# Order of the weight differences in a down projection, and of the token sums ahead of it

## The chip, the cores and the metric

The kernel runs on one core of one Trainium2 chip. The metric is the device time of one execution in microseconds (us); the median of several runs counts. Five engines work side by side and meet through semaphores: TensorE (PE) multiplies matrices, VectorE (DVE) and GpSimd (POOL) do elementwise work, ScalarE (ACT) does casts, copies and activations, and SyncE (SP) issues most transfers. Each engine works through its own queue in order, so an instruction that waits holds up all that stand behind it on that engine.

## The reference

The program computes two layers of a decoder trunk on 1024 tokens of width 1024. The change touches the dense feed-forward block that ends each layer:

```python
def swiglu(h, w_gate, w_up, w_down):
    return (jax.nn.silu(h @ w_gate) * (h @ w_up)) @ w_down

def reference(x, ...):
    h = x
    for layer in range(DEPTH):          # DEPTH = 2
        ...                             # norm and mixer, added to h
        n = rms_norm(h, norm2_g[layer])
        h = h + swiglu(n, ffn_w_gate[layer], ffn_w_up[layer], ffn_w_down[layer])
    return rms_norm(h, final_g)
```

All values are float32. The hidden width is 2816, that is 22 tiles of 128.

## The kernel before

**Exact products in three.** Every operand is cut into a high part (an ACT cast to the rounded matmul type) and a low part, the remainder (source minus high part, a subtraction on DVE or POOL). Each product is then three matmuls of 128x128 by 128x512: high by high, high by low, low by high. `vsplit` and `wsplit` do this for weights (low part on POOL, in `vsplit` always), `split` for activations (`pool_lo` chooses POOL or DVE for the low part). A DVE subtraction that forms such a remainder has line L358, a POOL one of a down weight L1370, its cast L1369.

**Seven products for eight.** The feed-forward block is multiplied in 2x2 blocks by a scheme of Winograd's kind: token halves are one side, neighbouring 128-wide feature tiles the other. With weight blocks a11, a12, a21, a22 the scheme needs S1 = a21 + a22, S2 = S1 - a11, a third difference a11 - a21 and a fourth one a12 - S2. On the activation side it needs four inner differences of each pair of hidden tiles.

**Early pairs.** The 22 hidden tiles are 11 pairs. For the first token half, `ffn_early` computes two products of each pair, for the gate and the up weights side by side: a half sum, which ACT copies out of PSUM into `u0` (line L1341 in `early`), and the full product, which the up weights' `up` in `uses` multiplies on DVE (L1241, kept as `last_up`). Meanwhile `form1` forms the sums and differences of the two token halves (`t1`, `t2`, `t3`, `t4`): `normed` (L1130) multiplies by the norm's factor `r` on DVE, `sub` (L1161) subtracts on DVE, `split` casts on ACT (L356) and forms the low part on DVE. `form1` is a generator; one step of it is written down after each early pair from pair 2 on.

**Late pairs.** `ffn_pair` computes the remaining five products of each pair. `form_down` forms the pair's four inner differences in its function `put` (line L1317, on DVE), splits them and stores them to `hc` in DRAM. For ten pairs that happens beside the next pair's products. The last pair's are written down inside `down`, as `rest`, in the first group, after its fourth product's operands are requested.

**Down projection.** `down` runs over three groups of hidden pairs (four, four and three pairs). In each group four pairs of output column tiles (`dps`) go through seven products in a fixed order: the plain first one, then S2, then a12 with the plain odd tiles (operand `ha` in the first group), the third difference, a22, S1 and the fourth difference. In a first loop S1 and S2 of all four are formed by `op`, which is `vop` on DVE (L1396); the loops of the second and third product form the third differences (`W[dp][2]`, in the place of a21) and the fourth (`W[dp][0]`, in the place of S2). The same line L1396 adds finished products to the residual `h`.

**Who sets the order.** The program is written in one order, but a planner places every engine's instructions by its own timeline: of what is ready it takes what comes first in the program, and what is ready early can be placed far ahead of its place in the program. `keep` fixes a transfer's place. `behind(i, first)` makes the planner put instruction `i` behind `first`; here it is used between instructions of one engine and adds no semaphore.

Of the kernel before, what the change touches and what calls it, by code (L numbers as in the profile page):

```python
# [13 lines left out]
ALU = mybir.AluOpType  # L14
# [9 lines left out]
NP = FT // 2  # L24
# [180 lines left out]
class Kern:  # L205
# [147 lines left out]

    def split(self, src, hi, lo, pool_lo=True):
        nc = self.nc
        nc.scalar.copy(hi, src)  # L356
        e = nc.gpsimd if pool_lo else nc.vector
        e.tensor_tensor(out=lo, in0=src, in1=hi.bitcast(F32), op=ALU.subtract)  # L358


    def rstd(self, h, r, tag="y"):
# [765 lines left out]
        return self.rstd(self.kt(self.h[hf]), self.t(pool, [P, HT], "rs", 1), tag)  # L1127

    def normed(self, out, hf, k, g, r):
        self.nc.vector.scalar_tensor_tensor(  # L1130
            out=out, in0=self.kt(self.h[hf])(k), scalar=self.col(g, k), in1=r, op0=ALU.mult, op1=ALU.mult
        )

# [7 lines left out]
                self.nc.sync.dma_start(self.bd[kk], f)  # L1141
                self.split(f, *self.X[nm][k], False)

    def form1(self, g, r, n8, cb, ft):

        nc = self.nc
        V = nc.vector
        X = self.X
        for nm in ("t1", "t2"):
            X[nm] = [self.hl(n8, k + 4 * (nm == "t1")) for k in range(4)]  # L1150
        for nm in ("22", "t4", "t3"):
            X[nm] = [[self.t(cb, [P, HT], "cb", 24, F32R) for _ in range(2)] for k in range(4)]
        n = 0

        def tmp():
            nonlocal n
            n += 1
            return self.t(ft, [P, HT], "ft", 4) if n % 2 else self.t(self.pp, [P, HT], "nq", 4)

        def sub(o, x, y):  # L1160
            V.tensor_tensor(out=o, in0=x, in1=y, op=ALU.subtract)  # L1161
            return o

        for k in range(4):
            b11, b21, b12, b22, t2 = (tmp() for _ in range(5))
            nc.sync.dma_start(b11, self.bd[k])
            nc.sync.dma_start(b21, self.bd[k + 4])
            self.normed(b12, 1, k, g, r)
            self.normed(b22, 1, k + 4, g, r)
            t1 = sub(b11, b12, b11)  # L1170
            self.split(sub(t2, b22, t1), *X["t2"][k], False)
            self.split(t1, *X["t1"][k], False)
            yield
            self.split(sub(b12, b22, b12), *X["t3"][k], False)
            self.split(sub(b21, b21, t2), *X["t4"][k], False)
            self.split(b22, *X["22"][k], False)
            yield
# [134 lines left out]
    def form_down(self, L, p, x, ts):  # L1312

        nc = self.nc

        def put(i, o, a, b):
            nc.vector.tensor_tensor(out=o, in0=a, in1=b, op=ALU.subtract)  # L1317
            t = ts[i in (2, 3)]
            self.split(o, t[:, 0, :], t[:, 1, :], p < NP - 1)
            d = (self.hc[L][p, i - 1], t.bitcast(F32))  # L1320
            if p == NP - 2 and i > 2:
                self.owed.append(d)
            else:
                (nc.gpsimd if p == NP - 2 else nc.sync).dma_start(*d)
            return o

        tmp = lambda: self.t(self.pp, [P, HT], "nq", 4)
        yield
        t1 = put(1, x["11"], x["12"], x["11"])
        yield  # L1330
        t2 = put(2, tmp(), x["22"], t1)
        yield
        put(4, tmp(), x["21"], t2)
        yield
        put(3, tmp(), x["22"], x["12"])
        yield

    def early(self, ps, w, u0, use):

        self.prod(ps, w[0](), self.X["11"], True, False)  # L1340
        self.nc.scalar.copy(u0, ps)  # L1341
        yield
        self.prod(ps, w[1](), self.X["21"], False, True)
        use("11", ps)
        yield
# [53 lines left out]
    def down(self, L, fp, fz, rest, X, first):  # L1399


        op, S = self.vop, self.nc.scalar
        h0, h1 = (self.kt(self.h[hf]) for hf in range(2))
        dps = range(KT // 2)
        j, ends = len(X), []

        def place():
            nonlocal j
            i, j = j % 12, j + 1
            if i >= 8:  # L1410
                return self.t(fp, [P, 2, HT], "ha", 4, F32R)
            return self.t(self.nb, [P, 2, HT], "n8", 8, F32R)

        def plain(hf, f):
            return self.plain8(L, hf, f, place(), self.t(fp, [P, HT], "hr", 4))

        for gi, g in enumerate(DGROUPS):
            n, ps = g[1] - g[0], range(*g)
            ta, tb = ("fffy", "mmrc")[:: 1 - 2 * (gi % 2)]
            s1, u0, a1 = [], [], []  # L1420
            W = [self.wdown(L, 0, g, fp, "wd0", 5)]
            X = X or [plain(0, 2 * p) for p in ps]
            W += [self.wdown(L, 2 * i, g, fp, "wd0", 5) for i in (1, 2, 3)]
            for i in dps:
                W[i] += self.wdown(L, 2 * i + 1, g, fp, "wd1", 5)
            A = [self.pst(t, [P, HT]) for t in ta]
            first += [self.vsplit(W[dp][0]) for dp in dps[len(first) :]]
            cast = self.last_cast
            for dp in dps:
                a11, a12, a21, a22 = W[dp]  # L1430
                self.prod(A[dp], first[dp], X, True, False)
                u0.append(self.t(fz, [P, HT], "u0", 4))
                self.behind(S.copy(u0[dp], A[dp]), cast)
                s1.append(op(self.wsum(fp, n, 4, 8), a21, a22))
                if ends:
                    self.behind(self.last_vop, ends[dp])
                a1.append(a11)
                W[dp][0] = op(self.wsum(fp, n, 4, 8), s1[dp], a11, ALU.subtract)
            X = [self.sums8(L, p, 2, place()) for p in ps]
            B = [self.pst(t, [P, HT]) for t in tb]  # L1440
            for dp in dps:
                self.prod(B[dp], self.vsplit(W[dp][0]), X, True, False)
                y = op(self.t(fz, [P, HT], "y", 2), B[dp], u0[dp])
                op(h1(2 * dp), h1(2 * dp), y)
                op(W[dp][2], a1[dp], W[dp][2], ALU.subtract)
            X = [plain(0, 2 * p + 1) for p in ps]
            for dp in dps:
                self.prod(A[dp], self.vsplit(W[dp][1]), X, False, True)
                op(h0(2 * dp), h0(2 * dp), A[dp])
                op(W[dp][0], W[dp][1], W[dp][0], ALU.subtract)  # L1450
            X = [self.sums8(L, p, 3, place()) for p in ps]
            for dp in dps:
                self.prod(B[dp], self.vsplit(W[dp][2]), X, False, False)
                y = op(self.t(fz, [P, HT], "y", 2), B[dp], u0[dp])
                op(h1(2 * dp + 1), h1(2 * dp + 1), y)
            X = [self.sums8(L, p, 4, place()) for p in ps]
            while self.owed:
                self.keep(self.nc.sync.dma_start(*self.owed.pop(0)))
            for _ in rest:
                pass  # L1460
            for dp in dps:
                self.prod(B[dp], self.vsplit(W[dp][3]), X, False, True)
                op(u0[dp], B[dp], u0[dp])
                op(h0(2 * dp + 1), h0(2 * dp + 1), u0[dp])
            X = [self.sums8(L, p, 1, place()) for p in ps]
            X6 = [plain(1, 2 * p + 1) for p in ps]
            if g[1] == NP:
                yield
            A = [self.pst(t, [P, HT]) for t in ta]
            for dp in dps:  # L1470
                self.prod(A[dp], self.vsplit(s1[dp]), X, True, False)
                op(h1(2 * dp + 1), h1(2 * dp + 1), A[dp])
            ends, first = [], []
            for dp in dps:
                self.prod(A[dp], self.vsplit(W[dp][0]), X6, False, True)
                op(h1(2 * dp), h1(2 * dp), A[dp])
                ends.append(self.last_vop)
            X = ()
        yield
# [208 lines left out]
def trunk(tc, A, out):  # L1688
    with ExitStack() as ctx:
        K = Kern(ctx, tc, A, out)  # L1690

        pq, gb, nb, ch = K.mixer0()
# [51 lines left out]
        def early(L, sp, lo, hi, form=None, steps=1):  # L1744
            for p in range(lo, hi):
                K.lo = tc.nc.vector if form else tc.nc.gpsimd
                K.ffn_early(L, p, sp, "ff" if L and p < 6 else "fm")
                K.lo = tc.nc.gpsimd
                for _ in range(steps if form else 0):
                    next(form, None)  # L1750


        gs, sp = K.pool("sp", "right")
        K.form0("n2a", K.factor_of(0, sp, "m"), K.n8(K.pp), sp)
        K.h[1] = K.wout(1, ch, K.s8(hy, "h1", 2), 2)
        gc, cb = K.pool("cb", "right")
        gt, ft = K.pool("ft", "left")
        r = K.factor_of(1, sp, "c")
        early(0, sp, 0, 2)
        early(0, sp, 2, NP - 1, K.form1("n2a", r, K.n8(nb), cb, ft))  # L1760
        close(gt)
        opened = late_open(0)
        early(0, sp, NP - 1, NP)
# [115 lines left out]
```

## Time and profile before

| | |
|---|---|
| median of 3 runs | 2348.12 us (2346.57 to 2348.34) |
| the profiled execution's own time | 2351.35 us |
| its span in the trace | 2349.6 us |
| mean granted clock of TensorE | 0.991 |
| PE busy | 2301.8 us, 98% of the span |
| DVE busy | 1703.8 us, 73% |
| ACT busy | 1055.7 us, 45% |
| POOL busy | 976.7 us, 42% |
| chain that ended last, by engine | PE 75%, DVE 10%, ACT 4%, DMA 4%, issue 4%, POOL 2% |

Times in the trace count from the start of the span. A row of a timeline gives the start, the duration, the engine, the line of the kernel, the operation, what is written and read (buffer numbers left out) and in brackets how long the engine sat idle before it and what ended that. Matmuls are pipelined, so a row of PE reads longer than the distance to the next one. In names, `ps_` tiles are PSUM, `w` and `wr` are split weights, `wd` raw down weights, `ws` formed weight sums, `hr` and `ha` raw and split hidden tiles.

### The profile page before, as it was taken

How to read it: one execution, taken by the hardware profiler on the slowest of the kernel's cores; microseconds unless marked ns; L12 is line 12 of the kernel's file. 1: busy time of each engine (PE TensorE's matmuls, PEld its weight loads, DVE VectorE, ACT ScalarE, POOL GpSimd, SP SyncE). 2: the span in 40 equal slices, each digit the busy share in tenths (PEclk: the TensorE clock that was granted, in tenths of full speed). 3: DMA queues.
4: the chain of work that ended last, by engine and by line, in shares of the span. 5: the costliest groups of instructions: out<-in, count | busy, mean ns of one | idle time of the engine just before them, and what ended most of it. 6: DMA issues, size and time to landing. Idle time of an engine off the chain costs nothing.

```text
span 2349.6 us, 35675 instructions
## 1 busy us (share of the span) xinstructions
PE 2301.8 (98%) x13056; PEld 1822.8 (78%) x13056; DVE 1703.8 (73%) x2667; ACT 1055.7 (45%) x1953; POOL 976.7 (42%) x764
## 2 busy tenths in 40 slices
PE   8999999999999999999999999999999999999998
PEld 6777777777777888888788887777688888887886
DVE  6876765866557548888876876887747788888767
ACT  5354533323555433333333455666735333333335
POOL 3122121211343057777677600002201677776775
PEclk9999999999999999999999999999999999999999
DMA  7565554443345645665685332123236566556763
GB/s 274 199 208 178 180 156 133 131 126 115 126 166 173 208 156 201 216 217 199 231 299 202 126 119 73 51 69 112 93 114 227 172 210 220 212 202 256 257 215 112
DMA packets 170622, 407.46 MB, mean 173 GB/s; under 512 B 43216, under 2 KB 45904, under 8 KB 170448
## 3 DMA queue, kind: packets, MB, share of 16 engines
q1 hardware_dynamic: 167040, 398.63, 49.5%
q10 hardware_dynamic: 2832, 4.45, 0.5%
q8 instruction: 104, 1.70, 0.3%
q0 software_dynamic: 576, 2.10, 0.2%
q14 instruction: 70, 0.57, 0.1%
HBM read 276.53 MB, written 123.21 MB: 170 GB/s over the span
## 4 chain that ended last, share of the span: by engine, by line
PE 75%; DVE 10%; ACT 4%; DMA 4%; issue 4%; POOL 2%; SPq 1%; DVEq 0%; ACTq 0%; POOLq 0%
PE ps_m L1182 7%; PE ps_m L1184 7%; PE ps_m L1183 7%; PE ps_f L240 7%; PE ps_m L240 5%; PE ps_f L350 4%; PE ps_f L352 4%; PE ps_f L351 4%; PE ps_f L1184 4%; PE ps_f L1183 4%; PE ps_f L1182 4%; PE ps_r L1182 2%; PE ps_r L1184 2%; PE ps_r L1183 2%; PE ps_c L1184 2%
## 5 line engine op out<-in xcount | busy, mean ns | idle before, releaser
L240 PE MATMUL ps_f<-n,w 128*128 128x512 f32 x1440 | 387.1, 416 | 10.4 <-ACT w L335 5.7
L240 PEld LDWEIGHTS ps_f<-n,w 128*128 128x128 f32 x1440 | 269.8, 193 | 95.3 <-issue 24.6
L336 POOL TENSOR_TENSOR w<-wr,w 128x512 fp32r<-128x512 f32 x63 | 86.7, 1384 | 524.3 <-ACT w L335 520.6
L335 ACT CAST w<-wr 128x512 fp32r<-128x512 f32 x231 | 141.1, 617 | 181.2 <-PE ps_f L352 70.3
L336 DVE TENSOR_TENSOR w<-wr,w 128x512 fp32r<-128x512 f32 x168 | 119.9, 717 | 56.8 <-ACT w L335 56.3
L336 POOL TENSOR_TENSOR w<-wq,w 128x512 fp32r<-128x512 f32 x91 | 130.4, 1444 | 31.4 <-ACT w L335 31.4
L1182 PE MATMUL ps_m<-n,w 128*128 128x512 f32 x333 | 130.7, 393 | 0.0
L1184 PE MATMUL ps_m<-n,w 128*128 128x512 f32 x333 | 129.8, 390 | 0.4 <-POOL w L1370 0.4
L1183 PE MATMUL ps_m<-n,w 128*128 128x512 f32 x333 | 129.6, 389 | 0.0
L352 PE MATMUL ps_f<-n,w 128*128 128x512 f32 x320 | 126.9, 397 | 0.6 <-POOL w L336 0.6
L350 PE MATMUL ps_f<-n,w 128*128 128x512 f32 x320 | 127.3, 399 | 0.1
L351 PE MATMUL ps_f<-n,w 128*128 128x512 f32 x320 | 126.9, 396 | 0.0
L1191 DVE TENSOR_TENSOR nq<-ps_m,u 128x512 f32<-128x512 f32 x88 | 58.8, 683 | 92.2 <-PE ps_m L1184 92.1
L1182 PE MATMUL ps_f<-n,w 128*128 128x512 f32 x287 | 113.9, 397 | 1.6 <-ACT u L1341 1.6
L1184 PE MATMUL ps_f<-n,w 128*128 128x512 f32 x287 | 112.1, 392 | 0.0
L1183 PE MATMUL ps_f<-n,w 128*128 128x512 f32 x287 | 111.8, 389 | 0.0
L358 POOL TENSOR_TENSOR n<-nq,n 128x512 fp32r<-128x512 f32 x60 | 100.0, 1679 | 7.6 <-ACT n L356 7.6
L1370 POOL TENSOR_TENSOR w<-wd,w 128x512 fp32r<-128x512 f32 (+1 forms) x62 | 85.9, 1393 | 39.6 <-ACT w L1369 37.9
L1182 PE MATMUL ps_m<-cb,w 128*128 128x512 f32 x236 | 91.9, 390 | 0.3 <-DVE nq L1191 0.3
L1183 PE MATMUL ps_m<-cb,w 128*128 128x512 f32 x236 | 91.8, 389 | 0.0
L1184 PE MATMUL ps_m<-cb,w 128*128 128x512 f32 x236 | 91.8, 389 | 0.0
L1370 POOL TENSOR_TENSOR w<-ws,w 128x512 fp32r<-128x512 f32 (+1 forms) x48 | 71.3, 1491 | 47.0 <-ACT w L1369 43.5
(520 smaller groups left out, 6472.9 us busy)
## 6 DMA issues: line engine op xcount, KB each, us to landing
hc<-n SPq DMA_DIRECT2D x84, 512.0 KB, 2.9
wsp<-w SPq DMA_DIRECT2D x54, 512.0 KB, 3.4
w<-wsp SPq DMA_DIRECT2D x54, 512.0 KB, 3.7
n<-hc SPq DMA_DIRECT2D x54, 512.0 KB, 5.7
wq<-in_w_gate SPq DMA_DIRECT2D x44, 512.0 KB, 4.4
u<-u SPq DMA_DIRECT2D x88, 256.0 KB, 2.9
wr<-in_w_in SPq DMA_DIRECT2D x34, 512.0 KB, 5.2
ha<-hc SPq DMA_DIRECT2D x34, 512.0 KB, 5.6
```

The source lines that it names most:

```text
L240: self.nc.tensor.matmul(out, lhsT, rhs, **kw)
L335: nc.scalar.copy(hi[:, :n], raw[:, c])
L336: self.lo.tensor_tensor(out=lo[:, :n], in0=raw[:, c], in1=hi.bitcast(F32)[:, :n], op=ALU.subtract)
L350: nc.tensor.matmul(ps, hi, rh, start=k == 0, stop=False)
L351: nc.tensor.matmul(ps, hi, rl, start=False, stop=False)
L352: nc.tensor.matmul(ps, lo, rh, start=False, stop=k == n - 1)
L358: e.tensor_tensor(out=lo, in0=src, in1=hi.bitcast(F32), op=ALU.subtract)
L1182: mm(ps, hi, xh, start=first and k == 0, stop=False, skip_group_check=True)
L1183: mm(ps, hi, xl, start=False, stop=False, skip_group_check=True)
L1184: mm(ps, lo, xh, start=False, stop=last and k == len(w) - 1, skip_group_check=True)
L1191: self.last_add = V.tensor_tensor(out=o, in0=x, in1=y, op=ALU.add)
L1370: nc.gpsimd.tensor_tensor(out=lo, in0=v, in1=hi.bitcast(F32), op=ALU.subtract)
```

## The change

Three orders are added.

In `down`, the third and the fourth differences of every group are put behind that group's last S2. The first group's last S2 is also kept as `self.s2`, and the four inner differences of the last pair, which `put` forms while the first group runs, are put behind it. In layer 0, the first product by `normed` in `form1` that belongs to the second token half is put behind the last early product of pair 1 on DVE, and the first token sum's cast (`t2`) behind pair 1's last copy of a half sum on ACT. Helpers return their instructions so that they can be named. Layer 1's `form1` is not changed.

```diff
     def split(self, src, hi, lo, pool_lo=True):
-        nc.scalar.copy(hi, src)
+        i = nc.scalar.copy(hi, src)
...
+        return i
...
-    def form1(self, g, r, n8, cb, ft):
+    def form1(self, g, r, n8, cb, ft, first=None):
...
-            self.normed(b12, 1, k, g, r)
+            i = self.normed(b12, 1, k, g, r)
+            if first and not k:
+                self.behind(i, first[0])
             self.normed(b22, 1, k + 4, g, r)
             t1 = sub(b11, b12, b11)
-            self.split(sub(t2, b22, t1), *X["t2"][k], False)
+            i = self.split(sub(t2, b22, t1), *X["t2"][k], False)
+            if first and not k:
+                self.behind(i, first[1])
...
         def put(i, o, a, b):
-            nc.vector.tensor_tensor(out=o, in0=a, in1=b, op=ALU.subtract)
+            j = nc.vector.tensor_tensor(out=o, in0=a, in1=b, op=ALU.subtract)
+            if p == NP - 1:
+                self.behind(j, self.s2)
...
-        self.nc.scalar.copy(u0, ps)
+        self.last_u0 = self.nc.scalar.copy(u0, ps)
...
                 W[dp][0] = op(self.wsum(fp, n, 4, 8), s1[dp], a11, ALU.subtract)
+            s2 = self.s2 = self.last_vop
...
                 op(W[dp][2], a1[dp], W[dp][2], ALU.subtract)
+                self.behind(self.last_vop, s2)
...
                 op(W[dp][0], W[dp][1], W[dp][0], ALU.subtract)
+                self.behind(self.last_vop, s2)
...
-        early(0, sp, 2, NP - 1, K.form1("n2a", r, K.n8(nb), cb, ft))
+        early(0, sp, 2, NP - 1, K.form1("n2a", r, K.n8(nb), cb, ft, (K.last_up, K.last_u0)))
```

More of the change, by code (lines that the diff above doesn't have):

```diff
@@ L1129, in normed @@
     def normed(self, out, hf, k, g, r):
-        self.nc.vector.scalar_tensor_tensor(
+        return self.nc.vector.scalar_tensor_tensor(
             out=out, in0=self.kt(self.h[hf])(k), scalar=self.col(g, k), in1=r, op0=ALU.mult, op1=ALU.mult
```

## The prediction

> **What bounds the kernel now.** I read the page first, then the stretches in which TensorE (PE) is not busy throughout, then the timelines of PE, VectorE (DVE), ScalarE (ACT) and GpSimd (POOL) around them, and the chain of waits.
>
> ```profile
> span 2349.6 us, 35675 instructions
> ```
> ```profile
> 1160.00:1170.00 10.00, 7.40 (x25) 5.20 (x24) 9.67 (x11) 3.33 (x6) 5.64 (x4) 0.85 1.03 416
> 2130.00:2140.00 10.00, 7.67 (x33) 5.81 (x32) 9.96 (x12) 3.46 (x6) 5.56 (x4) 1.00 1.03 414
> ```
> The two stretches (columns: window, length, busy time of PE, weight loads, DVE, ACT, POOL, then the granted clock) lie at the start of the down projection of layer 0 and of layer 1. PE works 7.4 and 7.7 of 10 us there, DVE 9.7 and 10.0. So inside these two stages DVE is the engine that has no room. In PE's timeline of layer 0 the stage looks like this:
>
> ```profile
> 1161.07 0.39 PE L1182 MATMUL ps_m<-n,w 128*128 128x512 f32 x1
> ...
> 1165.67 0.51 PE L1182 MATMUL ps_r<-n,wr 128*128 128x512 f32 x1 [1.90 <-ACT wr L1369]
> ...
> 1176.93 0.84 PE L1182 MATMUL ps_f<-ha,w 128*128 128x512 f32 x3
> ```
> The second product of the first group (the one with S2) begins at 1161.07 and the third (operand `ha`) at 1176.93: 15.86 us for 48 matmuls. It waits for ACT's cast of an S2. On DVE, in order:
>
> ```profile
> 1152.36 1.67 DVE L1317 TENSOR_TENSOR n<-n,n 128x512 f32<-128x512 f32 x1
> ...
> 1160.30 1.78 DVE L1396 TENSOR_TENSOR wd<-wd,wd 128x512 f32<-128x512 f32 x1
> ...
> 1176.03 1.77 DVE L358 TENSOR_TENSOR ha<-hr,ha 128x512 fp32r<-128x512 f32 x1
> ...
> 1185.29 0.69 DVE L1396 TENSOR_TENSOR h<-h,ps_f 128x512 f32<-128x512 f32 x1 [1.09 <-PE ps_f L1184]
> 1188.01 0.69 DVE L1396 TENSOR_TENSOR h<-h,ps_y 128x512 f32<-128x512 f32 x1 [2.03 <-PE ps_y L1184]
> ```
> The last two rows give PE's pace: one column tile, 12 matmuls, each 2.72 us, or 0.227 us a matmul. Four tiles should take 10.88 us, so the second product of layer 0 loses 4.98 us. The weight tiles of the stage, seen together:
>
> ```profile
> L1388 SPq DMA_DIRECT2D wd<-in_w_down x8: 327/378/430, 1134.7 to 1152.2; - x8
> L1369 ACT CAST w<-wd x5: 612/612/621, 1150.8 to 1173.6; 128x512 fp32r<-128x512 f32 x5
> L1370 POOL TENSOR_TENSOR w<-wd,w x4: 1296/1736/1747, 1151.7 to 1172.0; 128x512 fp32r<-128x512 f32 x4
> L1396 DVE TENSOR_TENSOR ws<-wd x4: 677/684/1752, 1157.0 to 1164.9; 128x512 f32<-128x512 f32 x4
> L1396 DVE TENSOR_TENSOR ws<-ws,wd x4: 679/686/694, 1157.8 to 1167.8; 128x512 f32<-128x512 f32 x4
> L1396 DVE TENSOR_TENSOR wd<-wd,wd x4: 677/682/1785, 1158.4 to 1168.4; 128x512 f32<-128x512 f32 x4
> L1396 DVE TENSOR_TENSOR ws<-wd,ws x4: 677/1224/1775, 1163.7 to 1170.8; 128x512 f32<-128x512 f32 x4
> ...
> DMA to landing us min/median/max: 3.6/5.1/6.4
> ```
> The four L1396 rows are the sum S1, then S2, the third difference and the fourth one, with min/median/max in ns and the first and last start. S2 of the fourth tile starts at 1167.8, 10 us after the first, because the other two kinds are mixed in between and the last pair's four inner differences (L1317, from 1152.36) stand ahead of all. One such operation takes 0.68 us alone and 1.78 us while POOL is in a subtraction:
>
> ```profile
> 1159.73 1.80 POOL L1370 TENSOR_TENSOR w<-ws,w 128x512 fp32r<-128x512 f32 x1 [4.56 <-ACT w L1369]
> ```
> The DVE row of 1160.30 starts inside it and ends 0.5 us after it. Layer 1 has the same order:
>
> ```profile
> 2133.30 0.39 PE L1182 MATMUL ps_m<-n,w 128*128 128x512 f32 x1
> ...
> 2147.08 0.39 PE L1182 MATMUL ps_f<-ha,wr 128*128 128x512 f32 x1
> ```
> 13.78 us for the same 48 matmuls, so 2.90 are lost. And in the chain of waits there:
>
> ```profile
> 2148.99 1.71 DVE ha L358
> 2150.70 0.04 issue
> 2150.75 0.50 PE ps_f L1183
> ```
> Even with the late start the third product has just met the next limit: the second remainder of `ha` that DVE forms. That row decides how much of the 2.90 and the 4.98 can be kept.
>
> **The early pairs.** PE stops once more, in layer 0's early pairs:
>
> ```profile
> 741.62 0.63 ACT L356 CAST n<-ft 128x512 fp32r<-128x512 f32 x1 [2.03 <-DVE ft L1161]
> ...
> 744.83 0.57 ACT L1341 COPY u<-ps_f 128x512 f32<-128x512 f32 x1
> ```
> ```profile
> 745.45 0.50 PE L1182 MATMUL ps_f<-n,w 128*128 128x512 f32 x1 [1.58 <-ACT u L1341]
> ```
> ```profile
> 737.21 0.75 DVE L1130 SCALAR_TENSOR_TENSOR ft<-h,pv,rs 128x512 f32<-128x512 f32 x1 [7.92 <-ACT rs L375]
> ...
> 755.43 0.68 DVE L1241 TENSOR_TENSOR sg<-sg,ps_m 128x512 f32<-128x512 f32 x1
> ```
> ACT stands at the cast of a token sum that DVE has not formed yet, and pair 1's copy of its half sum, for which PE waits 1.58 us, is queued behind it.
>
> **The change, part by part.** It adds no instruction, no transfer and no semaphore. Each new order is between two instructions of one engine, so only places in the DVE and ACT queues change.
>
> Token sums. The first two instructions of the formation go behind pair 1's last product on DVE (755.43 in this trace) and behind its last copy on ACT. The cast can no longer stand ahead of the copy, and 1.6 us of PE come back; the ends are 0 (another cast takes its place) and 1.6. The formation begins up to 18.2 us later (755.43 less 737.21). What hides that: the sums are used after pairs 2 to 10, each of 48 matmuls, so at least eight times 10.88 = 87 us. Without that cover it would cost the whole 18. The transfers that feed the formation are issued later with it, in the same queue as the weights of the early pairs; PE does not wait on those around here. I take 1.6.
>
> S2 first, layer 0. DVE is free at 1152.4, and the first S1 ran at 1157.0 without a wait, so its tile had landed by then; I take 1154.7, halfway. Eight operations at 0.68 are 5.4 us; two of them meet POOL, which adds 2 x 1.1. The fourth S2 is done at 1162.3 instead of 1168.5. The last tile cannot hinder this much: issued at 1152.2, landing after at most 6.4, it is there at 1158.6, and two operations after it end at 1160.0. The third S2 is done two operations earlier, at 1160.9; cast 0.61 and POOL 1.74 give 1163.3, where PE, which starts the third tile's matmuls early, wants it after eight matmuls, at 1162.9. That leaves 0.4 of the 4.98: the product ends at 1161.07 + 10.88 + 0.4 = 1172.4, 4.5 us sooner.
>
> The third product then. DVE still owes four third differences, four fourth ones and four inner ones; POOL is now busy without a pause, so I price each at 1.78. I assume that the third differences, which come before the splits of `ha` in the program, stand ahead of the first remainder and that the rest gives way except for two. First remainder: 1162.3 + 5 x 1.78 = 1171.2, in time. Second: 3 x 1.78 later, 1176.5. PE wants that after ten matmuls, at 1174.7, and waits 1.8; 38 matmuls remain, 8.6 us, so the product ends at 1185.1. Before it ended at 1176.93 + 10.88 = 1187.8. Layer 0 keeps 2.7 us, between 4.98 (no difference in the way) and below zero (all of them, see the first rival).
>
> Layer 1, moved by 2133.30 less 1161.07 = 972.2: second remainder at 2148.7, end 2157.3. Before: 2147.08 + 10.88 and the short wait at 2150.75, put at 0.3, give 2158.3. It keeps 1.0, between 2.9 + 0.3 and below zero.
>
> One part of the 4.98 needs a word. The clock column reads 0.85 in layer 0's window, 1.5 us of the ten, and 1.00 in layer 1's, with like waits in both; I count it as a consequence of the waits and as won back with them. [...]
>
> Groups two and three. There the third and fourth differences also go behind the last S2. The third ones are used one product after the next, two times 10.88 us away, against 4 x 1.78 = 7.1 us of work: no cost. Without that cover it would be 7.1 for each group. The four inner differences that are moved are used by the third group only; their casts, remainders and stores keep their places behind them.
>
> Sum: 1.6 + 2.7 + 1.0 = 5.3 us. The profiled execution took 2351.35 us (span 2349.6 and 1.75 around it) and would take 2346.1. It is 3.2 us above the median of the runs, 2348.12, from which I take the same 5.3: **2342.8 us**.
>
> **The rivals.** First, slower: the twelve differences pile up ahead of the remainders of `ha`. For it speaks that before the change all of them stand ahead of the second remainder (1176.03, after 1170.8), and that every pause of POOL which let DVE run at 0.68 was a pause in the S2 chain that now closes. With nine ahead, the second remainder is done at 1162.3 + 11 x 1.78 = 1181.9 and the third product ends at 1190.5, 2.7 us later than before; in layer 1 2162.7, 4.4 later. With all twelve it is 5.3 more in each, 8.0 and 9.7. The middle, 5.3 and 7.1, less the 1.6 of the early pairs, gives 2358.9; nine give 2353.6. It decides from the point where the second remainder ends after 1187.8 - 8.6 = 1179.2, nine operations past 1162.3, so with more than seven differences ahead (in layer 1, where the product must end by 2158.3, more than six). Against it: the splits of `ha` come in the program before the fourth and the inner differences, and an order by readiness and program place lets them pass. [...]
>
> Second, given back: the wait moves whole into the third product, which ends at 1187.8 and 2158.3 as before, with about seven differences ahead. Only 1.6 us remain: 2346.5. For it speaks the chain in layer 1, where PE already waits for that remainder.
>
> Third, the early order does not do what it says: the later formation and the weight splits of pair 2, both on DVE, collide and stop PE for as long as before. Then 3.7 us remain: 2344.4.
>
> **How the numbers follow.** A measurement of this kernel can tell about 0.2%, 4.7 us, from no change. The forecast has 0.48, the second and third rival 0.25 and 0.10, the first 0.17. With all stalls gone the gain is 1.6 + 4.98 + 3.2 = 9.8, so 2338.3; the range begins there, at 2338.0, and reaches over the second and third rival and their own spread to 2350.5, leaving out the first. Around the forecast alone it would be 2338.0 to 2343.4. Faster 0.48, same 0.35, slower 0.17.
>
> **What would show it.** Right: the eight S1 and S2 in one row on DVE, the fourth S2 done near 1162, the second product near 11 us long in both layers, the second remainder of `ha` done before 1179 by this trace's clock, and no PE wait at pair 1's copy. Wrong: a PE wait of more than 5 us inside the third product, with L1396 or L1317 rows of 1.7 us in an unbroken row ahead of L358 on `ha`; or a new wait of PE in pairs 2 to 4 of layer 0.

## The result, and the profile after

The changed kernel took 2356.3 us (median of 6 runs, 2353.61 to 2359.09) against 2348.67 for the kernel before (6 runs, 2346.57 to 2349.74). The ratio is 1.0031, with a 95% interval of 1.0020 to 1.0042: slower by 7.6 us, where 5.3 us less had been forecast. The profiled execution took 2353.61 us, the shortest of the six.

The stage windows of the changed kernel come first: layer 0's down projection in two rows, then layer 1's (window, length, busy time of PE, weight loads, DVE, ACT, POOL, then granted clock, DMA share and GB/s).

```profile
1160.00:1170.00 10.00, 7.08 (x32) 5.53 (x30) 9.97 (x7) 2.49 (x4) 10.00 (x6) 1.00 0.94 347
1170.00:1180.00 10.00, 7.07 (x20) 5.63 (x21) 10.00 (x14) 1.03 (x2) 3.05 (x3) 0.66 0.32 131
...
2140.00:2150.00 10.00, 6.38 (x25) 4.98 (x24) 9.96 (x7) 2.49 (x4) 9.32 (x6) 0.88 0.97 339
```
DVE has no room, as before, but now POOL has none either: 10.00 of 10 us with six operations. In the next ten PE gets a clock of 0.66. PE's timeline in layer 0 of the same execution:

```profile
1152.98 0.39 PE L1187 MATMUL ps_m<-n,w 128*128 128x512 f32 x1
...
1165.34 0.61 PE L1187 MATMUL ps_f<-ha,w 128*128 128x512 f32 x2
...
1166.70 0.39 PE L1189 MATMUL ps_f<-ha,w 128*128 128x512 f32 x1
1172.93 0.79 PE L1188 MATMUL ps_f<-ha,w 128*128 128x512 f32 x1 [5.84 <-DVE ha L358]
...
1184.80 0.39 PE L1187 MATMUL ps_m<-n,wr 128*128 128x512 f32 x1
```
The S2 product (1152.98 to 1165.34) takes 12.36 us instead of 15.86, so S2 does come earlier and PE gets it earlier. The third product (to 1184.80) takes 19.46 instead of 10.88, with one wait of 5.84 us for the first remainder of `ha` that DVE forms; ten matmuls behind it follow each other at 0.43 us instead of 0.227. DVE and ACT in the same stretch:

```profile
1151.29 0.69 DVE L1403 TENSOR_TENSOR ws<-ws,wd 128x512 f32<-128x512 f32 x1
1151.90 6.88 DVE L1403 TENSOR_TENSOR wd<-wd,wd 128x512 f32<-128x512 f32 x4
1158.70 3.47 DVE L1403 TENSOR_TENSOR ws<-wd,ws 128x512 f32<-128x512 f32 x2
1162.09 1.77 DVE L1322 TENSOR_TENSOR n<-n,n 128x512 f32<-128x512 f32 x1
1163.79 3.48 DVE L1403 TENSOR_TENSOR ws<-wd,ws 128x512 f32<-128x512 f32 x2
1167.19 1.75 DVE L1322 TENSOR_TENSOR nq<-n,n 128x512 f32<-128x512 f32 x1
1168.97 1.63 DVE L1322 TENSOR_TENSOR nq<-n,nq 128x512 f32<-128x512 f32 x1
1170.53 1.74 DVE L1322 TENSOR_TENSOR nq<-n 128x512 f32<-128x512 f32 x1
1172.19 1.28 DVE L358 TENSOR_TENSOR ha<-hr,ha 128x512 fp32r<-128x512 f32 x2
```
```profile
1156.09 2.57 ACT L356 CAST ha<-hr 128x512 fp32r<-128x512 f32 x4 [0.25 <-DMA hr<-hid]
```
The first row is the fourth S2. Behind it stand, without a gap, four third differences, four fourth and four inner ones: twelve in 20.3 us, 1.69 each. Only then come the two remainders of `ha`, whose casts ACT had finished at 1158.7. As far as their casts go, the remainders could have started 13 us sooner. Layer 1 shows the same on PE and DVE:

```profile
2148.25 0.80 PE L1188 MATMUL ps_f<-ha,wr 128*128 128x512 f32 x1 [3.62 <-DVE ha L358]
```
```profile
2144.78 1.75 DVE L1322 TENSOR_TENSOR nq<-n 128x512 f32<-128x512 f32 x1
2146.45 3.42 DVE L358 TENSOR_TENSOR ha<-hr,ha 128x512 fp32r<-128x512 f32 x2
```

To place the time I set the n-th of the 13,056 matmuls of one trace against the n-th of the other. Up to 740 us nothing is changed, and there the traces of this case stand up to 7.8 us apart; all differences below are counted from that point on, where they hold still except at named places. The changed kernel gains 1.9 at 742 us (the wait at pair 1's copy is gone), loses 1.4 near 978 us, loses 5.1 in layer 0's down projection (3.5 gained in the S2 product, 8.6 lost in the third) and 5.2 in layer 1's (1.2 gained, 6.4 lost): together +9.8. Between the two down projections the difference does not move by more than 0.1.

### The profile page after: what moved, and what is told of

Read it like the earlier page. It is cut to its first block, busy times and chain, and to the rows that moved or that the text cites. A ratio compares the mean times of both kernels' runs of the same rounds, so it can differ in the third digit from the quotient of the medians.

```text
span 2351.8 us, 35687 instructions
## 1 busy us (share of the span) xinstructions
PE 2299.2 (98%) x13056; PEld 1819.2 (77%) x13056; DVE 1713.7 (73%) x2667; ACT 1056.4 (45%) x1953; POOL 974.6 (41%) x764
## 4 chain that ended last, share of the span: by engine, by line
PE 77%; DVE 11%; ACT 4%; DMA 3%; issue 3%; POOL 1%; SPq 1%; DVEq 0%; ACTq 0%; POOLq 0%
PE ps_f L240 8%; PE ps_m L1187 7%; PE ps_m L1189 7%; PE ps_m L1188 7%; PE ps_m L240 5%; PE ps_f L350 4%; PE ps_f L352 4%; PE ps_f L351 4%; PE ps_f L1188 4%; PE ps_f L1189 4%; PE ps_f L1187 4%; PE ps_r L1189 2%; PE ps_c L1189 2%; PE ps_r L1188 2%; PE ps_c L1188 2%
## 5 line engine op out<-in xcount | busy, mean ns | idle before, releaser
L1196 DVE TENSOR_TENSOR nq<-ps_m,u 128x512 f32<-128x512 f32 x88 | 58.9, 684 | 92.1 <-PE ps_m L1189 92.0
```

The source lines that it names most:

```text
L1196: self.last_add = V.tensor_tensor(out=o, in0=x, in1=y, op=ALU.add)
```

## The experiments

The theory: all the loss is the pile of differences in front of the remainders of `ha`, each at 1.7 us because POOL subtracts at the same time. The rivals: the early order costs the time; or DVE and POOL are simply full, so that an order only chooses who waits.

| kernel | median us | ratio to before (95%) | from 740 us on, in its trace |
|---|---|---|---|
| changed | 2356.3 | 1.0031 (1.0020 to 1.0042) | +9.8 |
| token sums' order alone | 2347.08 | 0.9995 (0.9987 to 1.0004) | +0.8 |
| down orders alone | 2357.86 | 1.0043 (1.0030 to 1.0056) | +10.4 |
| third and fourth differences alone | 2351.87 | 1.0012 (1.0003 to 1.0020) | +3.9 |
| inner differences alone | 2355.9 | 1.0037 (1.0023 to 1.0050) | +6.1 |
| all behind the remainders | 2346.94 | 0.9997 (0.9989 to 1.0006) | -0.7 |
| third first, rest behind the remainders | 2344.98 | 0.9987 (0.9978 to 0.9996) | -3.3 |
| third first, rest behind the evictions | 2343.22 | 0.9982 (0.9973 to 0.9991) | +0.4 |
| changed, POOL fills instead of subtracting | 2340.14 | 0.9964 (0.9951 to 0.9977) | -8.3 |
| fourth differences last | 2342.09 | 0.9975 (0.9966 to 0.9984) | -2.1 |
| the same, only the cast ordered early | 2343.62 | 0.9985 (0.9975 to 0.9995) | -4.1 |
| the same, no early order | 2344.01 | 0.9980 (0.9971 to 0.9989) | -2.8 |

The medians of before that belong to the rows are 2348.67 (changed), 2347.9 (token sums alone, down orders alone, third and fourth alone, all behind the remainders), 2347.96 (inner alone, both with third first, fills) and 2348.66 (last three). A trace is one execution, a median five or more: where they lie far apart (rest behind the evictions, fourth last) the trace holds a late weight load, told below.

**Half of the change at a time.** The token sums alone:

```diff
         def put(i, o, a, b):
             j = nc.vector.tensor_tensor(out=o, in0=a, in1=b, op=ALU.subtract)
-            if p == NP - 1:
-                self.behind(j, self.s2)
...
                 op(W[dp][2], a1[dp], W[dp][2], ALU.subtract)
-                self.behind(self.last_vop, s2)
...
                 op(W[dp][0], W[dp][1], W[dp][0], ALU.subtract)
-                self.behind(self.last_vop, s2)
```


> Only the order of the token sums of layer 0 (behind pair 1's last copy and last product); the down projections are ordered as before the change. Theory (pile-up: the twelve differences stand ahead of the remainders of ha, and that is where all the loss is): the early pairs gain the 1.7 us that the two profiles show, so about 2347.0 against 2348.7 before. The wait of 1.66 us that appeared near 978 us in layer 0's late pairs hangs on which of DVE and POOL starts 0.05 to 0.2 us first; if it comes with the early order, 2348.4. Rival (the early order is the cost): about 2352 or more, with new PE waits in pairs 2 to 10.

Measured 2347.08, not to be told from before. (Its trace stands 0.4 under before up to layer 1's down projection; the 1.2 lost there come from slow matmuls and are told at the end.) The down orders alone are the other half:

```diff
-        early(0, sp, 2, NP - 1, K.form1("n2a", r, K.n8(nb), cb, ft, (K.last_up, K.last_u0)))
+        early(0, sp, 2, NP - 1, K.form1("n2a", r, K.n8(nb), cb, ft))
```

> Only the order in the down projections; the token sums are formed as before the change. Theory (pile-up): both layers lose what the changed kernel's profile shows, 5.2 each, so about 2348.7 + 10 = 2358 to 2359, with PE waits of 6 and 4 us inside the third product and DVE rows of 1.7 us in an unbroken row ahead of the remainders of ha. Rival (the early order is the cost): 2345 to 2349.

Measured 2357.86, with waits of 6.44 us in layer 0's third product and 3.57 in layer 1's. The loss is in the down orders; the early order is not the cause.

**The early half in its trace.** With the order PE does not stop at 742 us; without it, it does, 1.59 us for the copy. But in each of the seven traces with the whole early order a wait of 1.3 us stands near 978 us in layer 0's late pairs, and in none of the six without it. DVE, POOL and PE there, with the early order alone:

```profile
978.57 1.77 DVE L1322 TENSOR_TENSOR nq<-n 128x512 f32<-128x512 f32 x1
```
```profile
978.34 1.45 POOL L336 TENSOR_TENSOR w<-ws,w 128x512 fp32r<-128x512 f32 x1 [0.24 <-ACT w L335]
```
```profile
984.48 0.47 PE L1187 MATMUL ps_m<-n,w 128*128 128x512 f32 x1 [1.27 <-DVE u L1196]
```
and the same two operations with the down orders alone:

```profile
980.13 0.68 DVE L1322 TENSOR_TENSOR nq<-n 128x512 f32<-128x512 f32 x1
```
```profile
980.16 1.80 POOL L336 TENSOR_TENSOR w<-ws,w 128x512 fp32r<-128x512 f32 x1 [0.51 <-ACT w L335]
```
Where DVE starts 0.03 us before POOL it takes 0.68 and POOL waits; where POOL is 0.23 ahead, DVE takes 1.77, and the eviction behind it (`u`, L1196) is late for PE. All thirteen traces divide in this way: DVE takes 1.77 or 1.78 in the seven with the order and 0.68 in the six without. What shifts the two against each other by a quarter of a microsecond was not found; the order of PE's matmuls there is the same in both.

**Which differences cost.** Both kernels form the token sums as before the change. In the first only the third and fourth ones are ordered:

```diff
-            if p == NP - 1:
-                self.behind(j, self.s2)
```

> Only the third and fourth differences go behind the first group's last S2 (all groups); the last pair's four inner differences are unordered, as before the change, and so are the token sums. Theory (pile-up by number): the inner differences run at the stage's start, before the S2, and eight operations stand ahead of the remainders instead of twelve; the S2 product gains less, the third product loses less: 2349 to 2354, between before (2348.7) and the down order alone (2358). Rival (every difference costs, wherever it stands): no lower than the down order alone.

In the second only the inner ones are:

```diff
                 op(W[dp][2], a1[dp], W[dp][2], ALU.subtract)
-                self.behind(self.last_vop, s2)
...
                 op(W[dp][0], W[dp][1], W[dp][0], ALU.subtract)
-                self.behind(self.last_vop, s2)
```


> Only the last pair's four inner differences go behind the first group's last S2; third and fourth differences are unordered and the token sums are formed as before the change. Theory (pile-up: what counts is how many operations stand between the last S2 and the remainders of ha while POOL is busy): the four at 1.75 us each come after the mixed S2 and in front of the remainders, so the third product loses some of what it loses in the changed kernel and the S2 product gains some: 2350 to 2355, like the third and fourth differences alone (2351.9). Rival (the inner differences are harmless, they only fill idle DVE time): 2345 to 2348, a gain in the S2 product and no loss.

Measured 2351.87 and 2355.9, the second just above its bracket. In the traces +3.9 and +6.1, together 10.0 against 10.4 for both; in the medians 4.0 and 7.9 against 10.0. That the two add up is therefore shown only roughly. The four inner differences cost more than the eight others. They ran ahead of the S2 before the change, and run now where POOL is busy and PE is waiting; that this is the reason is likely, but no run isolates it. In layer 1's third product, with the third and fourth alone, then with the inner ones alone:

```profile
2151.47 0.50 PE L1188 MATMUL ps_f<-ha,wr 128*128 128x512 f32 x1 [3.00 <-DVE ha L358]
```
```profile
2150.98 0.79 PE L1188 MATMUL ps_f<-ha,wr 128*128 128x512 f32 x1 [4.32 <-DVE ha L358]
```

**POOL's part in the price.** The changed kernel with `vsplit`'s low part filled instead of subtracted (the low parts of the down weights are left out):

```diff
-        nc.gpsimd.tensor_tensor(out=lo, in0=v, in1=hi.bitcast(F32), op=ALU.subtract)
+        nc.gpsimd.memset(lo.bitcast(F32), 0.0)
```


> The changed kernel, with POOL's subtraction that makes the low part of each down weight tile replaced by a fill with zeros, which reads nothing (so the low parts of the down weights are left out of the product). The order on DVE stays: twelve differences ahead of both remainders of ha. Theory (the price of each difference is POOL's turn at reading and writing the buffers): the differences take 0.7 us instead of 1.75, the twelve about 8 to 9 us instead of 21, the remainders are done before PE wants them, and the waits of 6.2 and 4.0 us go: about 2340. Rival (the order by itself is what costs, or DVE's own rate): the differences keep 1.7 us, and the time stays near 2356.

Measured 2340.14. DVE, then POOL, in layer 0:

```profile
1158.16 2.49 DVE L1403 TENSOR_TENSOR wd<-wd,wd 128x512 f32<-128x512 f32 x4
1160.57 1.89 DVE L1403 TENSOR_TENSOR ws<-wd,ws 128x512 f32<-128x512 f32 x3
...
1164.37 1.60 DVE L1322 TENSOR_TENSOR nq<-n,nq 128x512 f32<-128x512 f32 x1
1165.89 1.77 DVE L1322 TENSOR_TENSOR nq<-n 128x512 f32<-128x512 f32 x1
1167.59 1.28 DVE L358 TENSOR_TENSOR ha<-hr,ha 128x512 fp32r<-128x512 f32 x2
```
```profile
1157.71 0.53 POOL L1377 MEMSET w<- 128x512 f32 x1 [2.19 <-ACT wr L1376]
1162.92 4.20 POOL L358 TENSOR_TENSOR ha<-hr,ha 128x512 fp32r<-128x512 f32 x2 [4.68 <-ACT ha L356]
...
1167.79 0.53 POOL L1377 MEMSET wr<- 128x512 f32 x1
```
The same twelve stand ahead of the same two remainders, but they take 9.4 us (1158.16 to 1167.59) instead of 20.3, and only the last two, which meet POOL's remainders of `ha`, cost 1.6 and more. PE does not wait in either third product. The price goes with what POOL does at the time: 1.69 each beside subtractions in the changed kernel, 0.64 each here for the two remainders of `ha` (1167.59), which run beside the fill of 1167.79. For most of the twelve, though, POOL is idle here (from 1158.24 to 1162.92), so this run shows that POOL's subtractions make the price; it does not show by what path, and it does not weigh a POOL that only writes against one with less to do. Part of the gain is POOL's own shorter path (0.53 instead of 1.3 for a weight tile): in the S2 product PE has no wait for a low part, where the changed kernel has 0.61 and 0.25.

**The order mended.** If the pile is the cause, the remainders must go first:

```diff
+        self.last_lo = e.tensor_tensor(out=lo, in0=src, in1=hi.bitcast(F32), op=ALU.subtract)
...
                 op(h1(2 * dp), h1(2 * dp), y)
+            X = [plain(0, 2 * p + 1) for p in ps]
+            if not gi:
+                s2 = self.s2 = self.last_lo
+            for dp in dps:
                 op(W[dp][2], a1[dp], W[dp][2], ALU.subtract)
                 self.behind(self.last_vop, s2)
-            X = [plain(0, 2 * p + 1) for p in ps]
```


> The whole change, but in the first group the four third, four fourth and the inner differences go behind the last remainder of ha that DVE forms, instead of behind the last S2. Theory (pile-up): the waits of 6.2 and 4.0 us in the third product go, and with them the 11 and 13 matmuls at half rate behind them (0.2 us each): 8.4 + 6.6 less than the changed kernel, about 2341.5, or 7 below before. Rival (given back: DVE and POOL are full in this stage, so the order only chooses which product waits): the wait moves to the fourth product, which needs the third differences, and the time is 2347 to 2352.

Measured 2346.94. The waits in the third product and the slow matmuls are gone in both layers, as the theory had it, but 5 us of the expected 15 did not come: the time lies 5.4 above the theory's 2341.5, at the lower end of the rival's range. PE's two new waits in layer 0:

```profile
1182.72 0.47 PE L1187 MATMUL ps_m<-n,wr 128*128 128x512 f32 x1 [0.90 <-ACT wr L1376]
...
1189.30 0.47 PE L1187 MATMUL ps_r<-n,w 128*128 128x512 f32 x1 [0.89 <-DVE y L1403]
```
The fourth product waits for a cast and then for an eviction that DVE does late; the S2 product also waits a little. So the rival was right in part: some of the time was given back, one product later (in layer 1 with two small waits more, in the sixth and seventh product). Next, the third differences stay behind S2 (their loop back in its place), and only the rest goes behind the remainders (`self.last_lo` as above):

```diff
...
             X = [plain(0, 2 * p + 1) for p in ps]
+            if not gi:
+                s2 = self.s2 = self.last_lo
```

> The whole change, but in the first group the four fourth differences and the inner ones go behind the last remainder of ha on DVE; the third differences stay behind the last S2. (The run with all of them behind the remainders left two new waits of 1.2 us in the fourth product: one for a weight cast that hung on the third differences, one for DVE's evictions of the S2 product.) Theory (pile-up; DVE has idle time between the last S2 and the arrival of ha, which the third differences fit into): the first of the two waits goes, the second stays: 1.2 us less in each layer, about 2344.5. Rival (DVE and POOL are full, the order only chooses who waits): the remainders end 4 to 7 us later and PE waits in the third product; 2347 or more.

Measured 2344.98; both waits of the fourth product are gone in layer 0 and layer 1, where the second was expected to stay. Small ones (0.29 to 0.40 us) stand in layer 0's sixth and seventh product instead. Then the rest behind the last sum of the S2 product into `h`:

```diff
                 op(h1(2 * dp), h1(2 * dp), y)
+                ev = self.last_vop
...
             X = [plain(0, 2 * p + 1) for p in ps]
+            if not gi:
+                s2 = self.s2 = ev
```

> As the kernel with the third differences first, but the four fourth differences and the inner ones go behind the last eviction of the S2 product (the sum into h), so behind the remainders too. Theory: both new waits of the fourth product go, so both layers keep what the S2 product gains: 0.5 (early pairs, net) + 3.9 (layer 0) + 3.0 (layer 1) less than before, about 2340.5. Rival (given back): the twelve evictions and differences meet the fourth product's casts on POOL and the wait moves on to the fifth or later products, 2345 to 2348.

Measured 2343.22, 2.7 short of the expected. Its trace has waits elsewhere: small ones in layer 1's sixth and seventh product, and in layer 0 a late load of a weight tile, for which the third S1 waits; the S2 behind it and the fourth S1 and S2 then run beside POOL, at 1.65 to 1.77 us each:

```profile
1151.13 0.69 DVE L1403 TENSOR_TENSOR ws<-wd 128x512 f32<-128x512 f32 x1 [2.02 <-DMA wd<-in_w_down]
```
Such a second wait of DVE for a tile, about 2 us long, is in this trace and in those of the next kernel and its copy without the early order, but not in the copy with only the cast ordered, which has the same order on DVE here. Whether it belongs to the order or to the execution stays open. Last, inner differences behind the remainders (`self.s2` is `self.last_lo`) and fourth ones behind the third product's sums:

```diff
                 op(h0(2 * dp), h0(2 * dp), A[dp])
+            if not gi:
+                s2 = self.last_vop
+            for dp in dps:
                 op(W[dp][0], W[dp][1], W[dp][0], ALU.subtract)
                 self.behind(self.last_vop, s2)
```


> The whole change, but in the first group the inner differences go behind the last remainder of ha on DVE and the four fourth differences behind the third product's last sum into h; the third differences stay behind the last S2. (In the two kernels before this one PE still lost 1.9 us in one layer each, in the sixth product, waiting 0.3 us at a time for loads of ha, and 0.4 us for a sum into h.) Theory (those loads stand in the queue behind the stores of the last pair's inner sums, so the inner differences must not come too late, and only the fourth differences can): no wait in the sixth product, 1.9 less than with all of both behind the remainders (2345.0) or behind the evictions (2343.2): 2341 to 2343. Rival (the small waits come from how the transfers happen to fall, not from the order): 2343 to 2346.

Measured 2342.09, ratio 0.9975 (0.9966 to 0.9984): 6.6 us under before, the lowest of the kernels that form the whole product, though its interval overlaps those of the kernels next to it. DVE in layer 1:

```profile
2125.85 4.67 DVE L1403 TENSOR_TENSOR wd<-wd,wd 128x512 f32<-128x512 f32 x4
2131.90 3.27 DVE L358 TENSOR_TENSOR ha<-hr,ha 128x512 fp32r<-128x512 f32 x2 [1.38 <-ACT ha L356]
2135.09 1.78 DVE L1322 TENSOR_TENSOR n<-n,n 128x512 f32<-128x512 f32 x1
...
2152.16 4.71 DVE L1403 TENSOR_TENSOR ws<-wd,ws 128x512 f32<-128x512 f32 x4
```
DVE reaches the remainders before ACT has cast them, and the fourth differences run 20 us later, when nobody waits for them. No wait is left in the sixth product here, but the two kernels below, with the same order, show such waits again in one layer each (0.25 to 0.32 us each). That the order removes them is therefore not shown.

**The early half once more.** On the best kernel, only the cast ordered:

```diff
             if first and not k:
-                self.behind(i, first[0])
+                pass
```

> As the kernel with the fourth differences last, but of the token sums only the first cast on ACT is ordered (behind pair 1's last copy); the first formation on DVE is free again, as before the change. Theory (PE waited 1.6 us because a cast stood ahead of the copy on ACT): the wait near 742 us goes with this half of the order alone, the same 1.9 us up to pair 4; what becomes of the wait near 983 us is open, 0 or 1.4 us. So the same time as the kernel with the fourth differences last, or 1.4 less. Rival (DVE's formation stood in the way of the eviction too): the wait near 742 stays in part, 1 us more.

A miss: the wait stays, 1.23 us of 1.6, as the rival had it. ACT, then PE:

```profile
739.28 0.62 ACT L356 CAST cb<-ft 128x512 fp32r<-128x512 f32 x1 [2.63 <-DVE ft L1162]
739.80 0.62 ACT L335 CAST w<-wr 128x512 fp32r<-128x512 f32 x1
740.49 1.14 ACT L356 CAST cb<-nq 128x512 fp32r<-128x512 f32 x2
741.53 0.58 ACT L1348 COPY u<-ps_f 128x512 f32<-128x512 f32 x1
```
```profile
742.16 0.50 PE L1187 MATMUL ps_f<-n,w 128*128 128x512 f32 x1 [1.23 <-ACT u L1348]
```
The ordered cast went behind the copy, and three other casts of the same formation took its place in front. So the copy is not free without the order on DVE, which holds the whole formation back; that order without the cast's was not run. With that half missing the wait at 978 us is absent too. Then the best kernel without the early order at all:

```diff
-        early(0, sp, 2, NP - 1, K.form1("n2a", r, K.n8(nb), cb, ft, (K.last_up, K.last_u0)))
+        early(0, sp, 2, NP - 1, K.form1("n2a", r, K.n8(nb), cb, ft))
```

> As the kernel with the fourth differences last, with the token sums formed as before the change. Theory: PE waits 1.98 us near 742 again and does not wait 1.66 us near 983, together 0.5 us more than the kernel with both orders. Rival (the early order is worth its whole 1.9): 1.9 us more. No difference of these sizes shows in the median of runs for certain; the profile shows it.

Measured 2344.01 against 2342.09 with the early order: too near to tell apart. The trace shows the wait at 742 us back and the one at 978 us gone, as expected.

## Why the prediction was wrong

**The early pairs: right in size, half in its cause.** 1.9 us came instead of 1.6, the formation was hidden, and no pair behind it waited. That one cast stood in the way was wrong (all casts of the formation did), and the 1.4 lost at 978 us was not seen: 0.5 is left.

**S2 first: right in the order, short in size.** The eight S1 and S2 stand in one row. The trace of after runs 8.1 us ahead of before's at this place, so its fourth S2, done at 1151.98, is at 1160.1 by before's clock; 1162.3 was forecast. The S2 product takes 12.36 us against the forecast 11.3, and 12.63 in layer 1, where 1.2 us were gained instead of 2.5. The forecast lacked two waits of PE for POOL's low parts of S2 (0.61 and 0.25 us in layer 0, 0.71 and 0.27 in layer 1).

**The step that failed: "I assume that the third differences, which come before the splits of `ha` in the program, stand ahead of the first remainder and that the rest gives way except for two."** Four were put ahead of the first remainder and six ahead of the second; twelve stand ahead of both. The argument was the place in the program. Why the planner chose otherwise is not shown: its own timeline is not on record, and by the trace ACT was done with `ha` at 1158.66, when eight of the twelve had not begun. The trace of before carried the warning, which the first rival named: there too all twelve stand ahead of the second remainder, and ahead of the first as well. By before's clock the second remainder was forecast for 1176.5 and came at 1181.6. But PE stopped earlier, at the first one, which was forecast for 1171.2, in time, and came at 1181.0. The third product was to end at 1185.1 and ended at 1192.9. With a wait of 5.84 us behind an unbroken row of differences, the prediction's own sign of being wrong is there.

So the number of differences ahead did not change. What changed is when DVE began and what each cost. In layer 0, the first remainder before the change, then DVE's first S1 after it:

```profile
1172.54 1.77 DVE L358 TENSOR_TENSOR ha<-hr,ha 128x512 fp32r<-128x512 f32 x1
```
```profile
1146.24 0.94 DVE L1403 TENSOR_TENSOR ws<-wd 128x512 f32<-128x512 f32 x1 [2.00 <-DMA wd<-in_w_down]
```
Before, the twenty operations (inner differences, S1, S2, third and fourth) took from 1152.36 to 1172.54, 20.2 us. After, they take from 1146.24 to 1172.19, 26.0 us, and begin 2.0 later by before's clock, because DVE waits for a weight tile where it formed the inner differences before. Together the first remainder starts 7.7 us later, while PE wants it 3.5 us sooner.

The runs that move the differences behind the remainders, and the one that makes them cheap, take the loss away; that is shown, not argued. And as the kernel with the fourth differences last ends 6.6 us under before, the time was not merely moved from one product to another.

**The rival's price.** With all twelve ahead it gave 8.0 and 9.7 us of loss; 5.1 and 5.2 were measured. In layer 0 the terms were too dear: the S2 done 2.2 earlier than forecast, a difference at 1.69 instead of 1.78 (1.1 for twelve), a remainder at 0.64 instead of 1.78 (2.3 for both, since POOL had run out of work by then: its last subtraction there ended at 1171.72). One was missing: the ten slow matmuls behind the wait, about 2 us. 8.0 - 2.2 - 1.1 - 2.3 + 2.0 is 4.4, near the 5.1. In layer 1 the S2 was done 3.1 earlier than forecast, the twelve took 18.2 us instead of 21.4, and thirteen slow matmuls added about 2.6: 9.7 - 3.1 - 3.2 + 2.6 is 6.0, against 5.2.

**The clock.** The prediction's 1.5 us at the lower clock are, in the trace of before, eight matmuls from 1166.93 on, 0.42 us each instead of 0.227. That they would go with the waits is borne out where the waits went: the six runs without a wait over 0.72 us in layer 0's S2 product (the changed kernel, down orders alone, remainders first, third first, fills, only the cast) have no slow matmul there. It is no proof, as two runs with waits much like before's (third and fourth alone 0.72 and 1.91, no early order 0.55 and 1.80) have none either. In the changed kernel the new waits in the third products (5.84 and 3.62 us) had ten and thirteen matmuls at 0.43 us behind them.

**Groups two and three: right.** Nothing was lost there.

**The chances.** 0.48 stood on an order inferred from the place in the program, 0.17 on the one that the trace of before showed. The range left out the first rival, and with it the outcome.

## What to carry to other kernels

An order "behind X" says nothing about what the moved work then stands in front of: list everything on that engine between X and the next instruction that another engine waits for, and put moved work behind that instruction, not behind X. Here a difference on DVE took 0.68 us alone and 1.69 in a row beside POOL's subtractions, so where a change closes the pauses of one engine, price moved work on its neighbour by the rows where both are busy, not by an average. Near 978 us DVE led POOL by 0.03 us or came 0.23 behind it, and the second cost PE 1.3 us: where two engines meet this closely, read their order again after a change far upstream.

## What the runs showed of the hardware

PE's clock after a wait did not follow from the wait's length alone. In the down projections the five waits of 3.57 us and more (5.84 and 3.62 in the changed kernel, 6.44 and 3.57 with the down orders alone, 4.32 with the inner differences) each had matmuls 0.43 us apart instead of 0.227 behind them, after the 3.57 only from 1.3 us later on; a wait of 3.0 had none. But two shorter waits, one shortly after the other, had them in some executions and not in others. Layer 1's window and waits with the early order alone:

```profile
2130.00:2140.00 10.00, 7.66 (x26) 5.59 (x25) 8.81 (x11) 3.89 (x8) 6.24 (x5) 0.83 0.77 309
```
```profile
2131.30 0.49 PE L1189 MATMUL ps_m<-n,w 128*128 128x512 f32 x1 [0.43 <-POOL w L1375]
...
2133.70 0.50 PE L1187 MATMUL ps_r<-n,w 128*128 128x512 f32 x1 [1.91 <-ACT w L1374]
```
and the same two matmuls before the change, whose window, shown in the prediction, reads 1.00:

```profile
2135.02 0.50 PE L1184 MATMUL ps_m<-n,w 128*128 128x512 f32 x1 [0.43 <-POOL w L1370]
...
2137.43 0.50 PE L1182 MATMUL ps_r<-n,w 128*128 128x512 f32 x1 [1.90 <-ACT w L1369]
```
Waits alike to 0.01 us, clock 0.83 against 1.00. So the length of the waits alone did not set the clock; what did is not shown.
